# GDN triangular inverses: square transposes on VectorE in place of two trips through DRAM, block matmuls in fixed halves, a shorter queue ahead of them

## The chip, the cores and the metric

The kernel runs on one core of a Trainium2 chip. The metric is the device time of one execution in microseconds (us), lower is better. TensorE (PE) does the matmuls, VectorE (DVE) and ScalarE (ACT) the elementwise work, GpSimd (POOL) a few fills with constants, and SyncE (SP) issues most DMAs. Every engine takes its own instructions in the order in which the program lists them.

## The reference, cut to what matters

Two layers of a flow-matching backbone over 512 latent and 256 context tokens. Each layer has one input projection, three mixers (a convolution module, neighbourhood attention, a gated DeltaNet called GDN), a gated merge and a convolutional feed-forward part. The change touches only the GDN, which is computed chunk by chunk, in two directions and for 4 heads:

```python
diff = g[..., :, None] - g[..., None, :]
decay = jnp.where(incl, jnp.exp(jnp.where(incl, diff, 0.0)), 0.0)
kb = k * beta
lmat = jnp.where(strict, jnp.einsum("bhnid,bhnjd->bhnij", kb, k) * decay, 0.0)
sol = lax.linalg.triangular_solve(lmat, rhs, left_side=True, lower=True, unit_diagonal=True)
```

The reference solves with a unit triangular matrix for each chunk, head and direction. The kernel works with chunks of 128 tokens and computes the inverse of each such 128x128 matrix, which the scan over the chunks then multiplies with.

## The kernel before

The program is written once per layer, and a planner then lists each engine's instructions in an order of its own, from the data that each needs and from the order in which the code was written. `issue_after(x)` adds an edge: what is written inside, on x's engine, is listed behind x.

**The GDN stage.** `gdn_core` is called twice in each layer, for two heads each time. In this document A0 and B0 are the two calls of layer 0, A1 and B1 those of layer 1. One call does the following in turn:

- For each head: matmuls `kk` (k with k) into PSUM, decay tiles `D` on VectorE and ScalarE, then `E` = kk times beta times D on VectorE (24 units in E: 2 directions, 2 heads, 6 chunks), and `A` = qk times D.
- `gdn_inverse(E)`: each unit of E is a 128x128 triangular matrix with four diagonal blocks of 32x32, each 32 partitions by 32 columns. These blocks go out to DRAM (L1031) and come back with one block per partition in `Eb` (L1032 to L1034). VectorE inverts them by a recursion of 31 pairs of instructions (`Tm` L1041, `Tt` L1043) on 112 partitions. The inverses are copied into transposed order (L1046 to L1048), go out to DRAM (L1050, L1051) and come back as 32x32 blocks into `Td` and `E` (L1058, L1059); ScalarE copies some into `TA` (L1060).
- Then block matmuls put the 32x32 inverses together to 64x64 (`iy` L1069, copied to `Y` by ScalarE, then `it` and `ir`), and those to 128x128 (`iy` L1101, `ir` L1110), with copies by ScalarE and VectorE between.
- The scan over the six chunks (`ch`), with v and k from tiles `tk` that are loaded behind the inverse, `kd` being scaled k. Then the output: norm, transposes `oT`.

**Filler.** Other mixers' projections (`na`, `pjl`, `pjc`) wait in a queue. `self.fill(us)` writes as many of their matmuls as take that many microseconds by a count of columns. `FILL` has these amounts for each place and layer: `e` behind each group of kk, `sub` behind the recursion, `y32` and so on behind the block matmuls, `a` to `d` in the scan, then those in the attention. What is left is written behind the attention, in `finish`. Filler's weights come by SP (`raw`), are rounded by ScalarE (`whi`) and split by VectorE (`wlo`); `nrm` reductions on VectorE and `ev`, `nsq` on ScalarE finish its units.

**Conv taps.** Instructions `ca` on VectorE, from another mixer, may be listed behind the end of the second recursion of a layer (in layer 1 the first ten behind that of the first).

**Buffers.** Tag D has three buffers of 1024 elements in a partition; D, Eb, Tt, Tf and tk share them.

Of the kernel before, what the change touches and what calls it, by code (L numbers as in the profile page):

```python
# [32 lines left out]
FILL = (dict(e=3.5, sub=37.6, y32=1.6, t32=2.5, y64=1.3, t64=1.0, a=0.4, b=0.45, c=0.4, d=0.59, out=1.5, x=3.7, pre=2.5, att=2.1),  # L33
        dict(e=4.1, sub=38.3, y32=1.0, t32=2.5, y64=1.69, t64=1.7, a=0.4, b=0.68, c=0.52, d=0.05, out=1.95, x=2.0, pre=2.08, att=1.41))
# [30 lines left out]
class Net:  # L65
# [955 lines left out]
    def gdn_inverse(self, E):  # L1021

        nc, V, S, T, gp = self.nc, self.nc.vector, self.nc.scalar, self.nc.tensor, self.gp
        de, dt, dR = self.d_e
        Eb = gp.tile([128, 1024], F32, tag="D", name="Eb", bufs=3)
        Tt = gp.tile([128, 1024], F32, tag="D", name="Tt", bufs=3)
        Tf = gp.tile([128, 1024], F32, tag="D", name="Tf", bufs=3)
# [35 lines left out]
        Y = gp.tile([128, 12, 64], F32, tag="Y", name="Y")  # L1063
        blk = lambda q, u, c: E[32 * q:32 * q + 32, u, 32 * c:32 * c + 32]
        yb = self.bank("iy")
        for u in range(12):
            for d in range(2):
                for s, t in prs[d]:
                    T.matmul(yb[32 * t:32 * t + 32, 32 * u:32 * u + 32], blk(s, 12 * d + u, t),  # L1069
                             Td[32 * s:32 * s + 32, 12 * d + u, :], start=True, stop=True)  # L1070
        self.fill(FILL[self.l]["y32"])
        Y1 = Y.rearrange("p a b -> p (a b)")[:, 0:384]
        S.activation(Y1, yb[:, 0:384], AF.Copy, scale=-1.0)
        Yq = lambda t, u: Y1[32 * t:32 * t + 32, 32 * u:32 * u + 32]
        tb, rb = self.bank("it"), self.bank("ir")
        for u in range(12):
            for d in range(2):
                for s, t in prs[d]:
                    if s // 2 == d:
                        T.matmul(tb[32 * t:32 * t + 32, 32 * u:32 * u + 32], blk(t, 12 * d + u, t), Yq(t, u),  # L1080
                                 start=True, stop=True)
                    T.matmul(rb[32 * s:32 * s + 32, 32 * u:32 * u + 32], Yq(t, u), blk(t, 12 * d + u, t),
                             start=True, stop=True)
        self.fill(FILL[self.l]["t32"])
# [446 lines left out]
```

## Time and profile before

| what | value |
|---|---|
| times of three runs | 2586.71, 2596.06, 2603.39 us |
| median | 2596.06 us |
| the profiled execution's own time | 2594.31 us |
| its span | 2592.5 us |
| mean granted TensorE clock | 0.983 |
| TensorE busy | 2494.4 us, 96% |
| VectorE, ScalarE busy | 1851.6, 1067.5 us |

The times of the views are from one profiled execution, counted from the start of its span. "Busy" means that at least one instruction of the engine is under way. Matmuls overlap, so a busy TensorE may still take in a new one only now and then; gaps, in contrast, are sure. [...]

### The profile page before, as it was taken

What the parts mean: (1) busy time and instruction counts of PE and PEld (TensorE: products, weight loads), DVE (VectorE), ACT (ScalarE), POOL (GpSimd) and SP (SyncE); (2) the same over time, 40 slices, a digit from 0 to 9 for tenths busy, and PEclk for the clock granted to TensorE, in tenths of its full rate; (3) what the DMA queues carried; (4) which work ended last, traced back from release to release, by engine and by line L of the source; (5) the groups of instructions that cost most, each with busy time, mean ns of one, the idle gap of its engine ahead of it and who ended that gap; (6) DMA issues with size and microseconds to landing.
All of it is one profiled execution on the core that took longest, in us unless ns stands there. A gap on an engine that the chain in (4) does not pass through costs nothing. (4 is left out here: it accounts for less than half of the span.)

```text
span 2592.5 us, 42262 instructions
## 1 busy us (share of the span) xinstructions
PE 2494.4 (96%) x16079; PEld 2156.6 (83%) x16079; DVE 1851.6 (71%) x4138; ACT 1067.5 (41%) x2159; POOL 8.4 (0%) x32
## 2 busy tenths in 40 slices
PE   6999999989999999999999999998989999999999
PEld 4889898967778888888888898887877778888887
DVE  6675578789679888776656477776768977755463
ACT  4564343445342244223223355634344543533242
POOL 0000000000000000000000000000000000000000
PEclk9999999999999999999999989998999999999999
DMA  7224434353458554453442342343446376322332
GB/s 253 91 76 137 138 99 140 98 177 109 149 186 270 179 176 125 121 161 115 150 135 87 110 141 95 120 134 112 146 125 211 100 251 188 130 90 98 98 98 90
DMA packets 207276, 356.77 MB, mean 138 GB/s; under 512 B 54832, under 2 KB 103200, under 8 KB 206944
## 3 DMA queue, kind: packets, MB, share of 16 engines
q1 hardware_dynamic: 182176, 320.97, 39.3%
q10 hardware_dynamic: 24896, 33.09, 3.6%
q8 instruction: 127, 2.08, 0.3%
q14 instruction: 77, 0.63, 0.1%
HBM read 297.31 MB, written 56.68 MB: 137 GB/s over the span
## 5 line engine op out<-in xcount | busy, mean ns | idle before, releaser
L132 DVE TENSOR_TENSOR wlo<-raw,whi 128x1024 fp32r<-128x1024 f32 (+2 forms) x319 | 385.4, 1209 | 292.3 <-ACT whi L131 289.1
L131 ACT CAST whi<-raw 128x1024 fp32r<-128x1024 f32 (+2 forms) x319 | 331.8, 1041 | 616.2 <-PE dn L150 197.7
L150 PE MATMUL upl<-hl,whi 128*128 128x512 f32 (+1 forms) x728 | 282.4, 389 | 2.4 <-ACT hl L322 1.9
L150 PE MATMUL upl<-ol,whi 128*128 128x512 f32 (+1 forms) x728 | 282.1, 388 | 0.0
L150 PE MATMUL upl<-hl,wlo 128*128 128x512 f32 (+1 forms) x728 | 280.9, 386 | 0.2 <-DVE wlo L132 0.2
L448 PE MATMUL pjl<-hl,whi 128*128 128x512 f32 x512 | 210.6, 411 | 7.6 <-ACT whi L131 7.6
L519 DVE SCALAR_TENSOR_TENSOR ca<-yp,caw,ca 128x783 f32<-128x783 f32 (+1 forms) x240 | 212.9, 887 | 6.7 <-ACT ca L512 4.6
L448 PE MATMUL pjl<-ol,whi 128*128 128x512 f32 x512 | 206.6, 404 | 0.0
L448 PE MATMUL pjl<-hl,wlo 128*128 128x512 f32 x512 | 206.2, 403 | 0.3 <-DVE wlo L132 0.2
L150 PEld LDWEIGHTS upl<-hl,whi 128*128 128x128 f32 x728 | 137.3, 189 | 30.7 <-ACT hl L322 2.1
L150 PEld LDWEIGHTS upl<-ol,whi 128*128 128x128 f32 x728 | 137.5, 189 | 30.0
L150 PEld LDWEIGHTS upl<-hl,wlo 128*128 128x128 f32 x728 | 137.4, 189 | 30.1 <-DVE wlo L132 0.7
L150 PE MATMUL dn<-fll,whi 128*128 128x512 f32 x352 | 139.0, 395 | 0.0
L150 PE MATMUL dn<-fhl,wlo 128*128 128x512 f32 x352 | 139.0, 395 | 0.0
L150 PE MATMUL dn<-fhl,whi 128*128 128x512 f32 x352 | 138.6, 395 | 0.1
L448 PEld LDWEIGHTS pjl<-hl,whi 128*128 128x128 f32 x512 | 97.8, 191 | 29.5 <-ACT whi L131 9.7
L448 PEld LDWEIGHTS pjl<-hl,wlo 128*128 128x128 f32 x512 | 97.6, 191 | 21.6 <-DVE wlo L132 1.2
L448 PEld LDWEIGHTS pjl<-ol,whi 128*128 128x128 f32 x512 | 98.0, 191 | 18.9 <-issue 0.5
L245 DVE CUSTOM_DVE_ANT_1 aj<-at,crows,par 128x512 f32<-128x512 f32 x128 | 93.1, 747 | 27.7 <-DMA at<-ada_t 16.0
L584 PE MATMUL na<-wlo,hl 128*128 128x256 f32 x384 | 108.9, 284 | 0.6 <-DVE wlo L132 0.6
L584 PE MATMUL na<-whi,hl 128*128 128x256 f32 x384 | 109.1, 285 | 0.0
L584 PE MATMUL na<-whi,ol 128*128 128x256 f32 x384 | 109.1, 284 | 0.0
(405 smaller groups left out, 6450.3 us busy)
## 6 DMA issues: line engine op xcount, KB each, us to landing
raw<-w_b SPq DMA_DIRECT2D x88, 512.0 KB
raw<-f_up SPq DMA_DIRECT2D x88, 512.0 KB
at<-ada_t SPq DMA_DIRECT2D x160, 256.0 KB
raw<-w_o SPq DMA_DIRECT2D x32, 512.0 KB
raw<-f_dn SPq DMA_DIRECT2D x32, 448.0 KB
raw<-w_a SPq DMA_DIRECT2D x24, 512.0 KB
mg<-mge ACTq DMA_DIRECT2D x48, 256.0 KB
raw<-w_br SPq DMA_DIRECT2D x24, 512.0 KB
```

What stands on the lines that cost most here:

```text
L131: self.nc.scalar.copy(hi[:, :n], r[:, :n])
L132: self.split = self.nc.vector.tensor_sub(lo[:, :n], r[:, :n], hi[:, :n]).ins
L150: self.nc.tensor.matmul(o, wk[a], x[k][b], start=(k == 0 and i == 0), stop=(k == n - 1 and i == 2))
L245: V.tensor_tensor_reduce(p, w, self.crows[:, r, 4 * h:4 * h + 4], 1.0, m if h else self.p(l, "adab")[:, t:t + 1], ALU.mult, ALU.add, accum ...
L448: self.nc.tensor.matmul(o, wk[a], x[k][b], start=(k == 0 and i == 0), stop=(k == n - 1 and i == 2))
L519: nc.vector.scalar_tensor_tensor(a, y[:, k:k + n], w[:, 31 * c + k:31 * c + k + 1], a, ALU.mult, ALU.add)
L584: self.nc.tensor.matmul(ps[:, :256], x[k][a], wk[b], start=(k == 0 and j == 0), stop=(k == 7 and j == 2))
```

## The change

The diagonal blocks no longer leave the chip. VectorE's transpose turns each 32x32 block of its operand by itself, which is what the blocks need: `Db` collects the diagonal blocks of E with the unit as the inner index (direction 1 through a transpose, direction 0 through a copy by ScalarE), one transpose of 128x1024 gives `Z`, with a unit in each partition. The recursion runs on `Z` and `W` over 128 partitions. Two more transposes give `X` and `Yt`, the inverses and their transposes in block form; the matmuls read them there, and copies put them into E and TA.

The block matmuls run in two halves of six units. A new helper `behind()` puts each group of them, and the filler written between groups (`inv`, 0.9 us each), behind the TensorE instruction written just before. `sub` goes from 37.6 and 38.3 to 22.0. X and Yt take the buffers of Db and Z, and the scan's tk loads take those of W, X and Yt. The tag `Td` of one later tile is renamed `sg`.

```diff
-FILL = (dict(e=3.5, sub=37.6, y32=1.6, t32=2.5, y64=1.3, t64=1.0, a=0.4, ...
-        dict(e=4.1, sub=38.3, y32=1.0, t32=2.5, y64=1.69, t64=1.7, a=0.4, ...
+FILL = (dict(e=3.5, sub=22.0, inv=0.9, t64=1.0, a=0.4, ...
+        dict(e=4.1, sub=22.0, inv=0.9, t64=1.7, a=0.4, ...
...
+    def behind(self):
+        eng = self.nc.tensor.engine
+        last = next((i for i in reversed(self.nc.cur_bb.bb.instructions) if i.engine == eng), None)
+        return self.tc.issue_after(last) if last is not None else ExitStack()
...
-        for b in range(4):
-            nc.sync.dma_start(de[b].rearrange("u (j i) -> j u i", i=32), E[32 * b:32 * b + 32, :, 32 * b:32 * b + 32])
-        nc.sync.dma_start(Eb[0:48], de[:, 0:12, :])
-        nc.sync.dma_start(Tf[64:112], de[:, 12:24, :])
-        V.tensor_copy(Eb[64:112], Tf[64:112, ::-1])
-        nc.sync.dma_start(Tt[0:112], self.A["eye32"][0:112])
+        nc.gpsimd.memset(cube(Db)[:, :, 24:32], 0.0)
+        nc.gpsimd.memset(W, 0.0)
+        nc.gpsimd.memset(W[:, ::33], 1.0)
+        for q in qs:
+            V.transpose(cube(Db)[q, :, 12:24].rearrange("p i u -> p u i"), E[q, 12:24, q])
+            S.copy(cube(Db)[q, :, 0:12].rearrange("p i u -> p u i"), E[q, 0:12, q])
+        V.transpose(Z, Db)
         for j in range(31):
...
         self.fill(FILL[self.l]["sub"])
-        S.copy(Mv[0:48], Tv[0:48].rearrange("p i c -> p c i"))
-        S.copy(Mv[64:112], Tv[64:112].rearrange("p i c -> p c i")[:, ::-1, ::-1])
-        V.tensor_copy(Tf[64:112], Tt[64:112, ::-1])
...
-            nc.sync.dma_start(Td[q], dt[b].rearrange("u (j i) -> j u i", i=32))
-            nc.sync.dma_start(E[q, :, q], dR[b].rearrange("u (j i) -> j u i", i=32))
-            S.copy(TA[q, :, 32 * (b % 2):32 * (b % 2) + 32], Td[q, 12 * d:12 * d + 12, :])
+        X, Yt = sq("X"), sq("Yt")
+        V.transpose(X, W)
+        V.transpose(cube(Yt), Wv.rearrange("p i c -> p c i"))
+        inv, ivt = (cube(Yt), cube(X)), (cube(X), cube(Yt))
...
+            for d in range(2):
+                us = slice(12 * d, 12 * d + 12)
+                (S.copy if d else V.tensor_copy)(E[q, us, q], ivt[d][q, :, us].rearrange("p i u -> p u i"))
+            S.copy(TA[q, :, 32 * (b % 2):32 * (b % 2) + 32], inv[d][q, :, 12 * d:12 * d + 12].rearrange("p i u -> p u i"))
...
+        def wait():
+            with self.behind():
+                self.fill(FILL[self.l]["inv"])
+
+        for u0, u1 in halves:
+            yb = self.bank("iy")
+            with self.behind():
+                for u in range(u0, u1):
+                    for d in range(2):
+                        for s, t in prs[d]:
+                            T.matmul(yb[32 * t:32 * t + 32, 32 * (u - u0):32 * (u - u0) + 32], blk(s, 12 * d + u, t),
+                                     inv[d][qs[s], :, 12 * d + u], start=True, stop=True)
+            S.activation(Y1[:, 32 * u0:32 * u1], yb[:, 0:192], AF.Copy, scale=-1.0)
+            wait()
```

The groups of `it` and `ir`, the second `iy` and the last `ir` are written in the same manner, with `wait()` behind each half of all but the last.

**TensorE, around the first iy of A0.** Before, 464 filler matmuls stand between the last qk and the first iy, and filler stands among the iy:

```order
L584 MATMUL na<-whi,ol_148 128x256
L584 MATMUL na<-whi,hl_149 128x256
L1069 MATMUL iy<-Td,E 32x32
L584 MATMUL na<-wlo,hl_149 128x256
L584 MATMUL na<-whi,ol_150 128x256
L584 MATMUL na<-whi,hl_151 128x256
```

Now 94 stand there (B0 174, A1 136, B1 250; before 453, 433, 349):

```order
L453 MATMUL pjl<-ol_149,whi 128x512
L453 MATMUL pjc<-oc_165,whi 128x256
L453 MATMUL pjl<-hl_148,wlo 128x512
L453 MATMUL pjc<-hc_164,wlo 128x256
L1085 MATMUL iy<-Yt,E 32x32 x2
L1085 MATMUL iy<-X,E 32x32 x2
```

The first iy has moved ahead of most of the filler, and all 24 iy of a half stand together, with six filler matmuls behind them.

**VectorE, from the last E of A0 to the recursion.** Before:

```order
L912 SCALAR_TENSOR_TENSOR E<-kk,beta,D 128x128 x4
L924 TENSOR_TENSOR A<-qk,D 128x256 x2
L592 TENSOR_REDUCE nrm<-nsq 128x4 x2
L132 TENSOR_TENSOR wlo<-raw,whi 128x1024
L488 SCALAR_TENSOR_TENSOR th<-th,pjl 128x512
L488 SCALAR_TENSOR_TENSOR th<-th,pjc 128x256
L132 TENSOR_TENSOR wlo<-raw,whi 128x1024
L1034 COPY Eb<-Tf 48x1024
L132 TENSOR_TENSOR wlo<-raw,whi 128x1024
L1041 TENSOR_TENSOR Tm<-Eb,Tt 112x31
```

Now:

```order
L917 SCALAR_TENSOR_TENSOR E<-kk,beta,D 128x128 x4
L929 TENSOR_TENSOR A<-qk,D 128x256 x2
L1040 STREAM_TRANSPOSE Db<-E 32x12x32 x4
L597 TENSOR_REDUCE nrm<-nsq 128x4
L1042 STREAM_TRANSPOSE Z<-Db 128x1024
L597 TENSOR_REDUCE nrm<-nsq 128x4
L1047 TENSOR_TENSOR Tm<-Z,W 128x31
L132 TENSOR_TENSOR wlo<-raw,whi 128x1024
L1049 TENSOR_TENSOR W<-W,Tm 128x31
```

The transposes follow the last A at once. Behind these rows the rest of A0's recursion stands without a break; in A1, B0 and B1 wlo and nrm stand among its steps.

**ScalarE, ahead of the first Y of A0.** Before:

```order
L594 DMA na_99<-ev 128x256
L1060 COPY TA<-Td 32x12x32
L1073 ACTIVATE Y<-iy 128x384
L955 ACTIVATE kd<-tk_3251,bd 128x128 x2
L1086 COPY TA<-it 32x12x32
L1087 COPY TA<-it 32x12x32
```

Now:

```order
L1064 COPY TA<-X 32x12x32 x2
L1062 COPY E<-Yt 32x12x32
L1064 COPY TA<-Yt 32x12x32
L1062 COPY E<-Yt 32x12x32
L1064 COPY TA<-Yt 32x12x32
L1062 COPY E<-Yt 32x12x32 x2
L1087 ACTIVATE Y<-iy 128x192
L960 ACTIVATE kd<-tk_3099,bd 128x128 x2
L1087 ACTIVATE Y<-iy 128x192
```

Eight copies stand together ahead of the first half's Y, and kd between the two halves.

## Rows read from the trace of the kernel before

**Rows 1.** The page, part 1: TensorE's busy time, share of the span, instructions.

```profile
PE 2494.4 (96%) x16079; PEld 2156.6 (83%) x16079; DVE 1851.6 (71%) x4138; ACT 1067.5 (41%) x2159; POOL 8.4 (0%) x32
```

**Rows 2.** Stages: window, length, busy PE PEld DVE ACT POOL, clock, DMA, GB/s.

```profile
229.70:300.90 71.20, 67.41 (x467) 62.05 (x466) 44.38 (x109) 22.93 (x36) 0.09 (x1) 1.00 0.46 134
300.90:322.90 22.00, 20.92 (x444) 19.13 (x444) 4.52 (x10) 9.25 (x22) 0.00 (x0) 1.00 0.54 148
374.10:441.40 67.30, 65.95 (x457) 61.04 (x457) 53.62 (x123) 20.32 (x31) 0.00 (x0) 1.00 0.40 118
441.40:458.00 16.60, 11.50 (x355) 10.49 (x355) 12.96 (x16) 6.65 (x15) 0.00 (x0) 0.79 0.69 187
1687.20:1757.70 70.50, 63.78 (x436) 58.69 (x435) 52.87 (x124) 24.12 (x41) 0.95 (x1) 0.95 0.47 138
1757.70:1774.10 16.40, 9.89 (x336) 9.08 (x336) 3.33 (x6) 6.58 (x14) 0.00 (x0) 0.50 0.70 198
1824.90:1894.40 69.50, 63.73 (x353) 55.20 (x352) 54.03 (x115) 21.31 (x28) 0.00 (x0) 1.00 0.49 146
1894.40:1916.00 21.60, 19.17 (x377) 16.06 (x377) 4.47 (x8) 7.79 (x16) 0.15 (x2) 0.84 0.60 170
sum 355.10, PE 322.35 PEld 291.73 DVE 230.19 ACT 118.95 POOL 1.20; mean PE 40.29 PEld 36.47 DVE 28.77 ACT 14.87 POOL 0.15
```

**Rows 3.** Timeline of VectorE at the end of A0's E: start, length, instruction.

```profile
226.87 1.11 DVE L912 SCALAR_TENSOR_TENSOR E<-kk,beta,D 128x128 f32<-128x128 f32 x4
...
238.32 0.74 DVE L924 TENSOR_TENSOR A<-qk,D 128x256 f32<-128x256 f32 x2
```

**Rows 4.** Timeline of TensorE in A0: last qk, the 94th filler, first iy.

```profile
229.10 0.28 PE L584 MATMUL na<-whi,hl 128*128 128x256 f32 x1
229.22 0.28 PE L584 MATMUL na<-wlo,hl 128*128 128x256 f32 x1
229.33 0.60 PE L920 MATMUL qk<-qT,kT 128*128 128x128 f32 x4
...
245.24 0.27 PE L448 MATMUL pjc<-hc,wlo 128*128 128x256 f32 x1
...
300.92 0.22 PE L1069 MATMUL iy<-Td,E 32*32 32x32 f32 x2 [2.16 <-issue]
```

**Rows 5.** VectorE by line, 243 to 301: xcount, busy, mean ns, idle before.

```profile
L1043 DVE TENSOR_TENSOR Tt<-Tt,Tm 112x31 f32<-112x31 f32 (+15 forms) x31 | 10.6, 342 | 0.9
L1041 DVE TENSOR_TENSOR Tm<-Eb,Tt 112x31 f32<-112x31 f32 (+15 forms) x31 | 10.6, 341 | 0.9
L132 DVE TENSOR_TENSOR wlo<-raw,whi 128x1024 fp32r<-128x1024 f32 x8 | 9.8, 1222 | 11.5 <-ACT whi L131 11.5
L592 DVE TENSOR_REDUCE nrm<-nsq 128x4 f32<-128x256 f32 x4 | 1.7, 416 | 3.5 <-ACT nsq L590 3.5
L1034 DVE COPY Eb<-Tf 48x1024 f32<-48x1024 f32 x1 | 0.7, 692 | 0.0
```

**Rows 6.** Timelines of VectorE and TensorE in A1: last E, the 136th filler.

```profile
1695.74 1.12 DVE L912 SCALAR_TENSOR_TENSOR E<-kk,beta,D 128x128 f32<-128x128 f32 x4
...
1705.29 0.39 PE L448 MATMUL pjl<-hl,whi 128*128 128x512 f32 x1
1705.52 0.39 PE L448 MATMUL pjl<-ol,whi 128*128 128x512 f32 x1
```

**Rows 7.** The same columns as rows 2, over B1's it and ir matmuls alone.

```profile
1908.20:1910.65 2.45, 1.86 (x144) 1.64 (x144) 0.00 (x0) 0.66 (x2) 0.00 (x0) 1.00 0.05 16
```

**Rows 8.** ScalarE's copies into TA: count, duration min/median/max in ns.

```profile
L1060 ACT COPY TA<-Td x16: 507/510/517, 300.8 to 1907.1; 32x384 f32<-32x384 f32 x16
```

**Rows 9.** As rows 2: A0's scan, and the attention of layers 0 and 1.

```profile
322.90:352.90 30.00, 29.98 (x240) 29.11 (x241) 22.64 (x73) 16.50 (x57) 0.00 (x0) 1.00 0.25 81
508.10:700.00 191.90, 182.94 (x1255) 144.36 (x1254) 161.16 (x331) 90.58 (x211) 0.41 (x6) 0.97 0.41 134
1962.00:2100.00 138.00, 130.05 (x854) 99.25 (x853) 117.89 (x293) 72.46 (x153) 0.31 (x4) 0.99 0.51 169
```

More of the change, by code (lines that the diff above doesn't have):

```diff
@@ L31 @@
 TAP_SPLIT = ((0, 0, 20), (10, 10, 40))
[L33 to L34 removed]
+FILL = (dict(e=3.5, sub=22.0, inv=0.9, t64=1.0, a=0.4, b=0.45, c=0.4, d=0.59, out=1.5, x=3.7, pre=2.5, att=2.1),
+        dict(e=4.1, sub=22.0, inv=0.9, t64=1.7, a=0.4, b=0.68, c=0.52, d=0.05, out=1.95, x=2.0, pre=2.08, att=1.41))
 K_ID, K_S1024, K_S32, K_N = 0, 128, 160, 192
@@ L1023, in gdn_inverse @@
         nc, V, S, T, gp = self.nc, self.nc.vector, self.nc.scalar, self.nc.tensor, self.gp
[L1024 to L1027, printed above, removed]
+        sq = lambda name: gp.tile([128, 1024], F32, tag="D", name=name, bufs=3)
+        cube = lambda t: t.rearrange("p (a b) -> p a b", b=32)
+        qs = [slice(32 * b, 32 * b + 32) for b in range(4)]
@@ L1064, in gdn_inverse @@
         blk = lambda q, u, c: E[32 * q:32 * q + 32, u, 32 * c:32 * c + 32]
-        yb = self.bank("iy")
-        for u in range(12):
+        Yq = lambda t, u: Y1[32 * t:32 * t + 32, 32 * u:32 * u + 32]
+        v = lambda x: x.rearrange("p (u c) -> p u c", c=32)
+        halves = [(6 * hh, 6 * hh + 6) for hh in range(2)]
+        def wait():
[11 more added lines that the diff above has]
+            wait()
@@ new lines, in gdn_inverse @@
+        for u0, u1 in halves:
+            tb, rb = self.bank("it"), self.bank("ir")
+            with self.behind():
+                for u in range(u0, u1):
+                    c = 32 * (u - u0)
+                    for d in range(2):
+                        for s, t in prs[d]:
+                            if s // 2 == d:
+                                T.matmul(tb[32 * t:32 * t + 32, c:c + 32], blk(t, 12 * d + u, t), Yq(t, u),
+                                         start=True, stop=True)
+                            T.matmul(rb[32 * s:32 * s + 32, c:c + 32], Yq(t, u), blk(t, 12 * d + u, t), start=True, stop=True)
+            S.copy(TA[32:64, u0:u1, 0:32], v(tb[32:64, 0:192]))
+            S.copy(TA[64:96, u0:u1, 32:64], v(tb[64:96, 0:192]))
@@ L1067, in gdn_inverse @@
             for d in range(2):
                 for s, t in prs[d]:
[L1069 to L1084, printed above, removed]
@@ L1085, in gdn_inverse @@
-        v = lambda x: x.rearrange("p (u c) -> p u c", c=32)
-        S.copy(TA[32:64, :, 0:32], v(tb[32:64, 0:384]))
-        S.copy(TA[64:96, :, 32:64], v(tb[64:96, 0:384]))
-        for d in range(2):
-            for s, t in prs[d]:
-                V.tensor_copy(E[32 * s:32 * s + 32, 12 * d:12 * d + 12, 32 * t:32 * t + 32], v(rb[32 * s:32 * s + 32, 0:384]))
+                    V.tensor_copy(E[32 * s:32 * s + 32, 12 * d + u0:12 * d + u1, 32 * t:32 * t + 32],
+                                  v(rb[32 * s:32 * s + 32, 0:192]))
@@ L1092, in gdn_inverse @@
+            wait()
         Y2 = gp.tile([128, 12, 64], F32, tag="Y", name="Y2")
@@ L1094, in gdn_inverse @@
         w = lambda x: x.rearrange("p (u c) -> p u c", c=64)
-        ybs, rbs = [], []
-        for hh in range(2):
+        for u0, u1 in halves:
             yb = self.bank("iy2")
-            for u in range(6 * hh, 6 * hh + 6):
-                for d in range(2):
-                    s, t = st(d)
-                    T.matmul(yb[t, 64 * (u - 6 * hh):64 * (u - 6 * hh) + 64], E[s, 12 * d + u, t], TA[s, u, :],
-                             start=True, stop=True)
-            S.activation(Y2[:, 6 * hh:6 * hh + 6, :], w(yb[:, 0:384]), AF.Copy, scale=-1.0)
-        self.fill(FILL[self.l]["y64"])
-        for hh in range(2):
-            rb = self.bank("ir2")
-            for u in range(6 * hh, 6 * hh + 6):
-                for d in range(2):
-                    s, t = st(d)
-                    T.matmul(rb[s, 64 * (u - 6 * hh):64 * (u - 6 * hh) + 64], Y2[t, u, :], E[t, 12 * d + u, t],
-                             start=True, stop=True)
+            with self.behind():
+                for u in range(u0, u1):
+                    for d in range(2):
+                        s, t = st(d)
+                        T.matmul(yb[t, 64 * (u - u0):64 * (u - u0) + 64], E[s, 12 * d + u, t], TA[s, u, :],
+                                 start=True, stop=True)
+            S.activation(Y2[:, u0:u1, :], w(yb[:, 0:384]), AF.Copy, scale=-1.0)
+            wait()
+        for u0, u1 in halves:
+            rb = self.bank("ir2")
+            with self.behind():
+                for u in range(u0, u1):
+                    for d in range(2):
+                        s, t = st(d)
+                        T.matmul(rb[s, 64 * (u - u0):64 * (u - u0) + 64], Y2[t, u, :], E[t, 12 * d + u, t],
+                                 start=True, stop=True)
             for d in range(2):
                 s, t = st(d)
-                V.tensor_copy(E[s, 12 * d + 6 * hh:12 * d + 6 * hh + 6, t], w(rb[s, 0:384]))
+                V.tensor_copy(E[s, 12 * d + u0:12 * d + u1, t], w(rb[s, 0:384]))
         self.fill(FILL[self.l]["t64"])
```

24 lines of the change are left out of this document (9 added, 15 removed).

## The prediction, on record before the result was known

> **What bounds the kernel now.** I read the page first. TensorE is busy 96% of the span, 98 us short of all of it [rows 1]. So what the kernel takes is TensorE's work plus its gaps, and a change that leaves its work alone (here: the same matmuls in the same number) can only move the gaps and the clock.
>
> Second view, the table by stage: each of the four inverses (layer 0 pairs A0 and B0, layer 1 pairs A1 and B1) cut in two. The first window of each runs from the last kk or qk matmul to the first block matmul iy; the reader is to see 71, 67, 71 and 70 us in which TensorE has nearly no gap. The second holds the block matmuls, 16 to 22 us. Over all eight, 355.10 - 322.35 = 32.8 us of gaps [rows 2]. That is all that can be won from gaps here. The granted clock adds a little: 16.6 us at 0.79, 16.4 at 0.50, 21.6 at 0.84 and 70.5 at 0.95 lose 3.5 + 8.2 + 3.5 + 3.5 = 18.7 us against the full level [rows 2].
>
> Third, the timelines, for who is late. In A0 the last A, which follows the last E on VectorE, is done at 239.06 [rows 3]; the first iy starts at 300.92 [rows 4]. These 62 us are the path of the old inverse: two trips through DRAM and the recursion. TensorE doesn't notice, since 464 queued matmuls stand in its order between the last qk and the first iy. An engine takes its instructions in order, so this count decides.
>
> **The change part by part.**
>
> *The path to iy gets shorter.* The trips, three copies of 48 partitions and the landing times go. What is left is a sum on VectorE, by the new order in A0: 4 transposes of 32x12x32, one nrm, one transpose of 128x1024, one nrm, one wlo, the 62 recursion steps, two transposes of 128x1024. The steps are 10.6 + 10.6 us busy and 1.8 us of gaps, 23.0 [rows 5]; they have 128 partitions in place of 112 and the same elements in each. nrm is 0.42, wlo 1.22 [rows 5]. No trace shows a square transpose: from below 0.69, the copy of 1024 elements, from above twice wlo; I take 1.15 for 1024 elements, just under wlo (as many elements, but one source in place of two) [rows 5], and 0.43 for 384. A0: 1.7 + 0.8 + 1.15 + 1.2 + 23.0 + 2.3 = 30.2 us from 239.06, so iy could start at 269.2, not 300.9. [...]
>
> *The queue in front gets shorter still.* FILL's sub goes from 37.6 and 38.3 to 22.0, and all block matmuls now stand behind the TensorE instruction written before them, so the planner can't pull filler of a later call ahead of iy within a unit. The new order has 94, 174, 136 and 250 filler matmuls between the last kk or qk and iy, where 464, 453, 433 and 349 stood. In A0 the orders of TensorE and VectorE are the same until the last E, so the trace of before says where TensorE will be: its 94th filler matmul starts at 245.24, done issuing at about 245.4 [rows 4]. It then waits for the transposes: 269.2 - 245.4 = **23.9 us idle**.
>
> A1 likewise: the last E is done at 1696.86, and TensorE has issued its 136 at about 1705.3 [rows 6]. The sum there has 7 nrm and 3 wlo: 1.7 + 2.9 + 1.15 + 3.7 + 23.0 + 2.3 = 34.7, so iy at 1731.6: **26.3 us idle**.
>
> In the B pairs the order ahead of the last E moves too, so I count from the last kk of the pair's first head. From there to the last A took 239.06 - 226.9 = 12.2 us in A0 (the first head's last E group starts at 226.87) [rows 3], and I use that. B0: 6 nrm and 4 wlo give 35.5, together 47.7; TensorE has 246 filler matmuls and 14 of kk and qk ahead of iy, 32.9 + 3.0 = 35.9 us (0.12 us for 256 columns, 0.23 for 512, the starts in [rows 4, 6]; 0.21 for a kk or qk, which the trace shows as two records: four records in 0.60 us end to end, and a new one each 0.11 [rows 4]): **11.8 us idle**. B1: 6 nrm, 3 wlo and a gate step of 0.7, 35.1, together 47.3, against 39.6 us of queue (275 filler matmuls and 10 of kk and qk): **7.7 us idle**. Together 69.7 us; small VectorE steps that also stand in the recursion (a tap, na_finish's thirteen) are left out and could only lengthen it.
>
> *Block matmuls in halves with filler between.* The gaps of the old second windows (1.1, 5.1, 6.5 and 2.4 us [rows 2]) go: while ScalarE moves one half out, TensorE has the other half and 1 us of filler. All 72 it and ir matmuls, 144 records, take 2.45 us [rows 7]; there are as many now, in the same order of blocks, so I add nothing for halving. One wait is added: eight copies into TA and E stand ahead of the first Y copy on ScalarE, 8 x 0.51 = 4.1 us [rows 8] and 0.3 for Y itself, against 0.8 + 1.0 + 0.8 + 1.0 = 3.6 us of TensorE's own work. About 1 us each time, 4 in all. Behind them stands kd, which needs the tk loads; their buffers are now the transposes' own, so SP issues them later. If a load lands after 5 us, the second Y copy is late by the excess; I cost it at nothing, since the filler of two more blocks stands behind.
>
> *The filler isn't saved, only moved.* It comes back in the chunk scan after the inverse, and behind the GDN part. In before the scan ran 30.0 us with 29.98 busy [rows 9]: no gap there to take it.
>
> *The sum:* 69.7 + 4 - 32.8 = +40.9 us. On the profiled execution (2594.31, its span 2592.5, 1.75 below the median of 2596.06) that is 2635.2; on the median 2637.0. I forecast **2637**.
>
> *The clock* I set at nothing: the four new block stages of some 14 us lose 3 each at 0.79, as one did, or 7 each at 0.50, as another did after its gaps [rows 2], 12 to 28 against 18.7 now: -7 to +9. [...]
>
> **The rivals.**
>
> *The path is hidden after all: faster.* If the queue in front covered the path, all 32.8 us of gaps and the 18.7 us of clock would be won: 2545. This decides at idle 0 in the four first windows. For it speaks that the path loses 32 us in A0. Against it: the 23.0 us of recursion alone [rows 5] cannot start before 239 in A0 nor end before 262, and TensorE is through its queue at 245.4 [rows 4].
>
> *The moved filler fills later gaps: no change.* TensorE has 9.0 us of gaps in layer 0's attention and 8.0 in layer 1's [rows 9]. If filler that comes later closed all of it, and the B pairs' idle didn't happen because VectorE is ahead there, the sum is 40.9 - 17 - 19.5 = +4: 2600; with either alone 2617 to 2620. For it speaks that some 30 us of filler now stand around layer 0's start of attention. Against it: those gaps wait for VectorE's softmax steps, and the filler set there per step is unchanged.
>
> *Worse than the sum.* If a transpose costs twice my price (5.2 us more in each inverse, 21) and the clock stays at 0.50 in the block stages (+9), with 10 us for what I left out: 2677.
>
> **How the numbers follow.** One per cent of 2596 is 26 us, about what can be told from no change: below 2570 is faster, above 2622 slower. My forecast's case, 2622 to 2677, has 0.66; the worse case beyond it 0.08; no change 0.19; faster 0.07. So faster 0.07, same 0.19, slower 0.74. The range goes down to 2605 (transposes at 0.69 give -8, the clock -7, later gaps closed -17) and up to 2677.
>
> **What would show it.** Right: TensorE in A0 and A1 idle for 20 to 30 us ahead of the first iy, ended by VectorE's Yt or X; less in B0 and B1; block stages of 14 to 17 us with 1 or 2 us of gaps; the transposes of 1024 elements at 0.7 to 1.3 us; the first iy of A0 near 269. Wrong: no such wait ahead of iy (the order doesn't hold on the chip, or VectorE's path is much shorter), or waits that appear as forecast while the gaps of the attention vanish. If transposes take over 2 us, only the size is off.

## The result, and the profile after

The changed kernel takes 2627.44 us (median of four runs, 2620.26 to 2636.10) against 2595.16 for the kernel before in the same comparison: a ratio of 1.012, 95% interval 1.0099 to 1.0141. It is **slower by 1.2%**, some 32 us. The profiled execution took 2636.1 us, its span 2634.2; it is the slowest of the four.

The first row to read is TensorE's, which answers to [rows 1].

```profile
PE 2485.9 (94%) x16079; PEld 2148.1 (82%) x16079; DVE 1884.2 (72%) x4190; ACT 1081.7 (41%) x2195; POOL 10.4 (0%) x40
```

As many matmuls as before. The span less TensorE's busy time is 2634.2 - 2485.9 = 148.3 us; it was 98.1. So 50 us of gaps have come, and the busy time fell by 8.5. The table by stage tells where. It has the windows of [rows 2]: A0, B0, A1, B1, each from the last kk or qk to the first iy and from there to the scan (window, length, then busy time of PE, PEld, DVE, ACT, POOL, granted clock, DMA share, GB/s).

```profile
232.20:273.90 41.70, 16.79 (x93) 14.21 (x92) 39.20 (x99) 10.32 (x16) 1.11 (x2) 0.72 0.11 38
273.90:291.30 17.40, 17.34 (x393) 14.74 (x394) 9.07 (x19) 10.07 (x20) 0.00 (x0) 0.88 0.53 152
366.40:403.60 37.20, 26.70 (x174) 24.02 (x172) 35.27 (x82) 11.06 (x20) 1.11 (x2) 0.92 0.23 75
403.60:421.10 17.50, 17.38 (x396) 14.98 (x397) 16.96 (x27) 10.91 (x21) 0.00 (x0) 0.88 0.52 168
1707.00:1754.20 47.20, 19.77 (x141) 18.50 (x142) 43.79 (x110) 12.94 (x23) 1.43 (x3) 0.73 0.21 70
1754.20:1778.10 23.90, 21.98 (x396) 17.05 (x397) 15.69 (x27) 11.68 (x22) 0.00 (x0) 0.82 0.41 133
1836.90:1879.40 42.50, 32.62 (x251) 31.33 (x249) 40.86 (x109) 14.31 (x26) 1.11 (x2) 0.92 0.26 85
1879.40:1901.90 22.50, 20.84 (x398) 16.57 (x399) 21.58 (x36) 11.26 (x22) 0.00 (x0) 0.93 0.36 113
sum 249.90, PE 173.43 PEld 151.40 DVE 222.43 ACT 92.55 POOL 4.76; mean PE 21.68 PEld 18.92 DVE 27.80 ACT 11.57 POOL 0.60
```

Length less PE in the four first windows is 24.9, 10.5, 27.4 and 9.9 us, together 72.7; VectorE is busy there for all but 1.6 to 3.4 us. In the four second windows it is 0.1, 0.1, 1.9 and 1.7, together 3.8. The sum of gaps is 76.5 where it was 32.8 [rows 2]: 43.7 of the 50.2 us stand here.

Who ended the wait in A0 is in the timelines. TensorE (start, length, instruction, idle time before it and what ended it):

```profile
247.81 0.80 PE L453 MATMUL pjl<-hl,wlo 128*128 128x512 f32 x1 [2.04 <-DVE wlo L132]
...
251.66 0.27 PE L453 MATMUL pjc<-hc,wlo 128*128 128x256 f32 x1
273.91 0.26 PE L1085 MATMUL iy<-Yt,E 32*32 32x32 f32 x2 [21.98 <-DVE Yt L1054]
```

VectorE, the path that ended it:

```profile
240.44 0.75 DVE L929 TENSOR_TENSOR A<-qk,D 128x256 f32<-128x256 f32 x2
241.11 3.50 DVE L1040 STREAM_TRANSPOSE Db<-E 32x384 f32<-32x384 f32 x4
...
244.98 1.24 DVE L1042 STREAM_TRANSPOSE Z<-Db 128x1024 f32<-128x1024 f32 x1
...
246.43 0.19 DVE L1047 TENSOR_TENSOR Tm<-Z,W 128x31 f32<-128x31 f32 x1
...
270.59 0.19 DVE L1049 TENSOR_TENSOR W<-W,Tm 128x31 f32<-128x31 f32 x1
270.82 1.25 DVE L1053 STREAM_TRANSPOSE X<-W 128x1024 f32<-128x1024 f32 x1
271.99 1.87 DVE L1054 STREAM_TRANSPOSE Yt<-W 128x1024 f32<-128x1024 f32 x1
```

From the last A's end (241.2) to iy it is 32.7 us, where 62 were needed before [rows 3, 4]. VectorE's part of the change does what it says; TensorE was given even less to do meanwhile.

### The profile page after: what moved, and what is told of

Its sections match the earlier page's. It is cut to its first block, busy times and chain, and to the rows that moved or that the text cites. A ratio compares the mean times of both kernels' runs of the same rounds, so it can differ in the third digit from the quotient of the medians.

```text
span 2634.2 us, 42216 instructions
## 1 busy us (share of the span) xinstructions
PE 2485.9 (94%) x16079; PEld 2148.1 (82%) x16079; DVE 1884.2 (72%) x4190; ACT 1081.7 (41%) x2195; POOL 10.4 (0%) x40
## 4 chain that ended last, share of the span: by engine, by line
PE 59%; DVE 14%; DMA 7%; ACT 3%; issue 2%; SPq 0%; ACTq 0%; DVEq 0%; POOL 0%
PE upl L150 18%; PE dn L150 10%; PE pjl L453 6%; PE upc L150 5%; DVE ca L524 4%; PE mbl L150 3%; PE na L589 3%; PE pjl L150 3%; DVE wlo L132 2%; PE og L623 1%; PE wo L150 1%; DMA at<-ada_t 1%; PE pjc L453 1%; DMA mg<-mge 1%; DVE W L1049 1%
## 5 line engine op out<-in xcount | busy, mean ns | idle before, releaser
L453 PE MATMUL pjl<-hl,whi 128*128 128x512 f32 x512 | 216.5, 423 | 4.0 <-ACT whi L131 4.0
L245 DVE CUSTOM_DVE_ANT_1 aj<-at,crows,par 128x512 f32<-128x512 f32 x128 | 93.3, 747 | 32.6 <-DMA at<-ada_t 17.7
```

The source lines that it names most:

```text
L245: V.tensor_tensor_reduce(p, w, self.crows[:, r, 4 * h:4 * h + 4], 1.0, m if h else self.p(l, "adab")[:, t:t + 1], ALU.mult, ALU.add, accum ...
L453: self.nc.tensor.matmul(o, wk[a], x[k][b], start=(k == 0 and i == 0), stop=(k == n - 1 and i == 2))
```

## The experiments

Ratios are to the kernel before on the same chip, with 95% intervals. "Gap" is a window's length less TensorE's busy time.

**The queue's length alone.** The changed kernel with the old numbers in FILL:

```diff
-FILL = (dict(e=3.5, sub=22.0, ...        dict(e=4.1, sub=22.0, ...
+FILL = (dict(e=3.5, sub=37.6, ...        dict(e=4.1, sub=38.3, ...
```

> The changed kernel with one thing undone: sub is 37.6 and 38.3 again, as in the kernel before; the transposes, the halves and the fixed order stay. Between the last kk or qk and the first iy then stand 208, 303, 253 and 273 filler matmuls (A0, B0, A1, B1), where the changed kernel has 94, 174, 136 and 250; by columns 31.9, 40.5, 35.0 and 46.0 us in place of 14.8, 24.4, 17.6 and 31.6. Theory Q (the loss is TensorE's idle ahead of iy, and that idle is the path on VectorE less the queue in front): idle falls from 24.9, 10.5, 27.4 and 9.9 to about 8, 0, 10 and 0 us, 55 us are won, and the time is about 2572. Rival T (the transposes, the strided copies or the halves cost the time themselves, and the queue only shows it): about 2627 as in the changed kernel, at best 2610. Rival M (filler that is taken ahead is missing later, in the scans and in the attention): the idle ahead of iy falls as in Q, but gaps of 20 us or more appear behind it, and the time is 2590 to 2600.

Measured: 2576.13, ratio 0.9918 (0.9892 to 0.9944). The first windows, columns as above:

```profile
228.20:274.60 46.40, 33.26 (x211) 29.37 (x210) 44.07 (x108) 15.81 (x23) 1.12 (x2) 0.91 0.28 93
363.30:408.50 45.20, 42.12 (x306) 39.46 (x304) 42.91 (x98) 17.95 (x29) 1.12 (x2) 1.00 0.30 102
1675.70:1724.50 48.80, 36.45 (x256) 33.71 (x254) 46.49 (x114) 16.59 (x29) 1.43 (x3) 0.95 0.32 103
1807.20:1856.90 49.70, 46.76 (x280) 41.02 (x279) 46.84 (x108) 23.02 (x33) 1.11 (x2) 1.00 0.35 114
```

Gaps 13.1, 3.1, 12.4, 2.9: 31.5 us in place of 72.7, and 51 us less time. Q expected 8, 0, 10 and 0; the waits that end at iy itself are 12.2, 0, 8.4 and 0, the rest are smaller waits within the queue. One entry of FILL turned the loss of 1.2% into a gain of 0.8%. Theory Q stands, T falls: transposes, halves and edges together are faster than what they replaced. M falls too: outside these windows the profile has 70.9 us of gaps, the changed kernel's 75.6. The gaps of these windows are 41 of the 51 us. In the profiles TensorE's busy time fell as well, from 2485.9 to 2468.6 us; some 6 us of that are a stretch at half speed, described in the last section, that one profile has and the other hasn't.

**The path's length alone.** The changed kernel with X and Yt computed three times over:

```diff
+        for _ in range(3):
-        V.transpose(X, W)
-        V.transpose(cube(Yt), Wv.rearrange("p i c -> p c i"))
+            V.transpose(X, W)
+            V.transpose(cube(Yt), Wv.rearrange("p i c -> p c i"))
```

> The changed kernel with X and Yt computed three times over (the same result), which adds 2 x (1.24 + 1.87) = 6.2 us to VectorE's path ahead of iy in each inverse and nothing else. Theory Q: TensorE waits there in all four pairs, so each microsecond of path is one of time: +25, 2652. Rival: if something else bounds the inverses (ScalarE's copies, the loads, filler that is due later), less than 10 us: 2627 to 2637.

Measured: 2646.80, ratio 1.0214 (1.0189 to 1.0239). Against the changed kernel that is 19 us by the medians, and 0.0094 of 2595, 24 us, by the ratios. The first windows of A0 and A1:

```profile
231.30:279.30 48.00, 17.41 (x101) 14.76 (x101) 45.48 (x105) 10.35 (x16) 1.12 (x2) 0.71 0.10 35
...
1712.60:1764.80 52.20, 18.48 (x139) 17.32 (x137) 49.83 (x115) 12.78 (x22) 1.43 (x3) 0.72 0.21 63
```

Gaps 30.6 and 33.7, up by 5.7 and 6.3 for 6.2 us of path; in B0 and B1 they are up by 5.6 and 5.8, together 23.3 us. While TensorE waits there, a microsecond of path is a microsecond of time, from the other side than the queue.

**The transposes taken back.** The kernel with sub 37.6 and 38.3, the diagonal blocks through DRAM again. The halves and the edges stay, but for the edge of the first half's iy, which goes; as many filler matmuls stand in front of it:

```diff
-        for q in qs:
-            V.transpose(cube(Db)[q, :, 12:24].rearrange("p i u -> p u i"), E[q, 12:24, q])
-            S.copy(cube(Db)[q, :, 0:12].rearrange("p i u -> p u i"), E[q, 0:12, q])
-        V.transpose(Z, Db)
+        for b in range(4):
+            nc.sync.dma_start(de[b].rearrange("u (j i) -> j u i", i=32), E[32 * b:32 * b + 32, :, 32 * b:32 * b + 32])
+        nc.sync.dma_start(Eb[0:48], de[:, 0:12, :])
...
-            with self.behind():
+            with (self.behind() if u0 else ExitStack()):
...
-                                     inv[d][qs[s], :, 12 * d + u], start=True, stop=True)
+                                     Td[qs[s], 12 * d + u, :], start=True, stop=True)
```

> The kernel of the run before with sub 37.6 and 38.3 (2576 us), in which the transposes alone are taken back: the diagonal blocks go through DRAM again as in the kernel before, the halves and the edges stay (the first iy has none, but as much filler in front: 208, 303, 253 and 273 matmuls). Theory Q with the path: the path from the last A to iy is some 62 us in place of 33, so iy comes about 25 to 29 us later in each pair, the queue in front covers no more than before, and idle ahead of iy grows by 25 to 29 us in A0 and A1 and by 15 to 25 in B0 and B1, 80 to 105 us in all: 2655 to 2680. Rival D (the trips are hidden anyway, and the transposes give nothing beside halves and edges): 2576 to 2590.

Measured: 2659.97, ratio 1.0269 (1.0236 to 1.0302). The first windows of A0 and B0:

```profile
227.80:295.40 67.60, 32.99 (x212) 29.38 (x211) 38.35 (x102) 14.27 (x20) 0.13 (x1) 0.78 0.35 104
385.80:449.60 63.80, 42.14 (x307) 39.47 (x305) 48.39 (x113) 14.61 (x24) 0.00 (x0) 0.87 0.39 117
```

Gaps 34.6 and 21.7 (29.6 and 20.1 in layer 1), with the very queue of the run with sub 37.6 and 38.3. In A0 33.8 us of them are one wait ahead of iy, which the DMA into Td ends. Behind a queue of this length the transposes are worth 84 us by the medians, 91 by the ratios. Rival D falls. The ratio says too what halves and edges do without the transposes: 2.7% slower than the kernel before, in which 464 and 453 filler matmuls stand where 208 and 303 stand here. The halves were in no run taken back by themselves.

**The trips with a queue long enough for them**, in layer 0:

```diff
-        self.fill(FILL[self.l]["sub"])
+        self.fill(FILL[self.l]["sub"][pr])
...
+FILL = (dict(e=3.5, sub=(66.0, 58.0), ...        dict(e=4.1, sub=(40.0, 36.0), ...
```

> The trips through DRAM with the halves and the edges (all of them), and a queue that is long enough for the trips in layer 0 alone: sub 66 and 58 there, 61.5 and 62.8 us of filler in front of iy by columns; 40 and 36 in layer 1 (36.7 and 43.6). Layer 0, from the first xT to the first upl, took 837.5 us in the kernel before, 831.9 with transposes and sub 37.6, and 875.7 with trips and sub 37.6. Theory Q: what counts is the path less the queue, so layer 0 takes 830 to 842 here, though the path is 30 us longer: where filler covers the trips the transposes give next to nothing. Layer 1 stays near the 659 of the run with trips and sub 38.3. In all about 2620. Rival P (the trips cost by themselves, through DMA or the extra copies): layer 0 at 850 or more.

Measured: 2669.02, ratio 1.0282 (1.0250 to 1.0313). A miss: layer 0 took 868.5 us (118.9 to 987.4), not 830 to 842. (The kernel before took 834.6 to its first upl, not the 837.5 of the expectation.) Its windows ahead of iy (A0, B0), then from the start of the attention to the first lnT, a matmul of the convolution module's norm, and from there to the first upl:

```profile
230.30:301.60 71.30, 63.95 (x437) 58.54 (x437) 43.70 (x108) 21.66 (x32) 0.18 (x1) 0.99 0.44 131
397.70:461.80 64.10, 64.10 (x408) 57.61 (x406) 51.04 (x105) 18.35 (x26) 0.00 (x0) 1.00 0.48 137
569.20:720.50 151.30, 123.75 (x878) 99.87 (x878) 131.53 (x253) 61.47 (x141) 0.41 (x6) 0.93 0.41 132
720.50:987.40 266.90, 246.05 (x1433) 204.67 (x1433) 215.61 (x543) 93.33 (x178) 0.00 (x0) 0.98 0.63 199
```

The idle ahead of iy went as Q has it (gaps 7.4 and 0.0). But the third window has 27.6 us of gaps, and 16.8 of them are one wait. TensorE's row, then the conv taps of layer 0 on VectorE here and in the run with transposes and sub 37.6 (count, ns min/median/max, first and last start):

```profile
720.53 1.09 PE L542 MATMUL lnT<-kc,lnx 128*128 128x128 f32 x4 [16.76 <-DMA lnx<-ca]
...
L525 DVE SCALAR_TENSOR_TENSOR ca<-yp,caw,ca x120: 1015/1029/1036, 444.6 to 714.1; 128x783 f32<-128x783 f32 x120
...
L524 DVE SCALAR_TENSOR_TENSOR ca<-yp,caw,ca x120: 1014/1028/1036, 399.4 to 655.1; 128x783 f32<-128x783 f32 x120
```

The taps stand behind the second recursion, and that ends 45 us later here. Their result comes back as lnx, and TensorE, which is through with what stands in front at 703.8, waits for it until 720.5; in the other run it reaches lnT at 713.6 and finds it there. Filler is not what was missing: 192 filler matmuls of this layer still stand behind the wait. Another 8.8 us of gaps in the last window are waits of wo for wlo. So a queue can cover a long path ahead of iy, and the path still costs: it holds up what VectorE has to do behind it. The time that rival P named (layer 0 at 850 or more) came; that the DMAs or the extra copies cost it by themselves, the rows don't show. No run had lnT behind the filler, which would settle how much of the miss this wait is.

**The edges alone.** `behind()` returns no edge, sub stays at 22.0:

```diff
-        return self.tc.issue_after(last) if last is not None else ExitStack()
+        return ExitStack()
```

> The changed kernel without the edges: behind() adds none, sub stays 22.0. The planner then pulls filler of later calls ahead of iy by itself: 271, 271, 310 and 296 filler matmuls stand there, 42.6, 37.1, 41.6 and 40.0 us by columns, and only 1.5 to 3.7 us of filler are left among the block matmuls (8 to 12 us with the edges). Theory Q: hardly any idle ahead of iy (0, 0, 3 and 2 us), but the gaps among the block matmuls come back, as many as in the kernel before (15 us) and up to 5 us more in each pair, since eight copies on ScalarE stand ahead of the first Y: 2627 - 68 + 11 to 31, that is 2570 to 2590. Rival T: about 2627 or more. If the pin is what loses the time, and not the number in FILL, this run and not the next shows it.

Measured: 2584.91, ratio 0.9949 (0.9930 to 0.9968). The loss turns into a gain of 0.5%, with the small number in FILL still there: the planner pulls other filler ahead of iy (271 to 310 matmuls), and the waits for iy are 0.9 to 1.6 us. So it is the edges that make the number count at that place. The block matmuls pay, as expected: in A0's and B0's second windows

```profile
278.40:294.80 16.40, 10.49 (x348) 9.90 (x349) 8.14 (x18) 9.99 (x19) 0.00 (x0) 0.69 0.47 144
390.40:402.80 12.40, 9.63 (x353) 9.06 (x354) 10.57 (x21) 9.60 (x20) 0.00 (x0) 0.86 0.50 155
```

there are 5.9 and 2.8 us of gaps (2.0 and 2.3 in layer 1); with the edges 0.1 and 0.1 (1.9 and 1.7).

**The small number without edges and transposes**, in the kernel before:

```diff
-FILL = (dict(e=3.5, sub=37.6, ...        dict(e=4.1, sub=38.3, ...
+FILL = (dict(e=3.5, sub=22.0, ...        dict(e=4.1, sub=22.0, ...
```

> The kernel before with sub = 22.0 and nothing else. In its planner's order 464, 453 and 433 filler matmuls still stand between the last qk and the first iy in A0, B0 and A1, as before, and 419 in B1 (349). Theory Q, in which the number of matmuls that stand there decides: no change, 2590 to 2600, and the first iy of A0 at 300 to 302 us. Rival S (the smaller number alone shortens the queue and loses time): 2610 to 2650.

Measured: 2640.54, ratio 1.0166 (1.0144 to 1.0189). A miss in the time: 2590 to 2600 was expected. At the place that Q speaks of nothing changed: first iy of A0 at 298.9, gap 2.95. The loss comes later. Layer 0, from its first xT to its first upl, takes 849.8 us where it took 834.6, layer 1 665.2 where it took 628.9; 9 us are won between the two. The windows: A0 ahead of iy, from B0's scan to the attention, from B1's scan to the attention, layer 1's attention.

```profile
228.30:298.90 70.60, 67.65 (x468) 62.24 (x467) 44.45 (x110) 22.96 (x36) 0.16 (x1) 1.00 0.45 135
...
488.80:526.90 38.10, 30.73 (x181) 26.64 (x180) 32.72 (x70) 13.37 (x40) 0.20 (x3) 0.96 0.47 150
...
1949.30:1974.90 25.60, 8.07 (x35) 5.75 (x33) 22.98 (x64) 5.66 (x21) 0.16 (x2) 0.67 0.34 113
1974.90:2121.50 146.60, 132.68 (x840) 103.13 (x841) 100.96 (x248) 65.58 (x139) 0.16 (x2) 0.94 0.44 146
```

The three last in the kernel before, whose first iy of A0 was at 300.92 [rows 4]:

```profile
488.20:524.50 36.30, 35.89 (x210) 31.04 (x209) 32.51 (x69) 13.47 (x40) 0.20 (x3) 1.00 0.46 149
...
1945.10:1971.40 26.30, 26.07 (x121) 21.07 (x119) 25.94 (x66) 10.19 (x27) 0.00 (x0) 1.00 0.52 181
...
1971.40:2081.70 110.30, 103.06 (x718) 77.67 (x719) 96.23 (x245) 58.70 (x129) 0.31 (x4) 0.98 0.46 151
```

The window between B1's scan and the attention holds 35 matmuls and 17.5 us of gaps, where 121 left 0.2. The planner, given less to put in front, took what stood there (419 ahead of B1's iy in place of 349), and TensorE waits for VectorE: 9.6 us for the attention's `ax`, 7.9 for the scaling of the scan's output. Behind B0 it is the same in small, 181 matmuls and 7.4 us of gaps, one wait for `ax`, where 210 left 0.4. Rival S has the size by a way that it didn't name. Why layer 1's attention then has 13.9 us of gaps in place of 7.2 (it also holds 122 more matmuls) stays open.

**Strides.** Db unit by unit, so that the small transposes write in one piece and Z reads with steps; then X and Yt too:

```diff
-            V.transpose(cube(Db)[q, :, 12:24].rearrange("p i u -> p u i"), E[q, 12:24, q])
-        V.transpose(Z, Db)
+            V.transpose(cube(Db)[q, 12:24, :], E[q, 12:24, q])
+        V.transpose(cube(Z), cube(Db).rearrange("p u i -> p i u"))
...
-        V.transpose(X, W)
-        V.transpose(cube(Yt), Wv.rearrange("p i c -> p c i"))
+        V.transpose(cube(X).rearrange("p u i -> p i u"), Wv)
+        V.transpose(cube(Yt).rearrange("p u c -> p c u"), Wv.rearrange("p i c -> p c i"))
```

> The changed kernel with the diagonal blocks collected unit by unit (each 32x32 result in one piece of memory), and the stride moved into the one transpose that makes Z. In the changed kernel the four transposes into Db (384 elements, writes 128 bytes apart) take 0.85 to 0.89 us each, those of 1024 elements in one piece 1.24, and Yt, which reads 128 bytes apart, 1.87. Theory stride (the step in memory costs): the four fall to about 0.46 (384/1024 of 1.24), ScalarE's copies into Db from 0.90 to about 0.5, and Z rises to about 1.87; in all 1.0 us less path in each inverse and iy as much earlier, 2627 - 4, not to be told from no change in time. Rival (small transposes have a fixed price): the four stay at 0.85 and more, Z rises, the path is 0.6 longer.

> The run above, and X and Yt are written unit by unit too, so that the copies into E and TA and the matmuls read in one piece, and the transposes carry every stride. Theory stride: X rises from 1.24 to about 1.87 (writes apart), Yt (both apart) from 1.87 to 2.5, ScalarE's eight copies fall from 0.85 to 0.51 (as the copies into TA from Td in the kernel before), VectorE's four from 0.67; the first Y copy starts some 2.7 us sooner behind iy. The block stages have hardly a gap in the changed kernel (0.1, 0.1, 1.9 and 1.7 us), so the time changes by less than 5 us: 2622 to 2632. Rival (the copies ahead of Y do hold TensorE up): 3 us won in each pair, 2615.

Measured: one run each, 2618.13 and 2622.71, not to be told from the changed kernel's 2620 to 2636. VectorE's groups in A0 of the second (line, engine, operation, count, busy us, mean ns, idle before):

```profile
L1040 DVE STREAM_TRANSPOSE Db<-E 32x384 f32<-32x384 f32 x4 | 2.3, 568 | 0.0
L1042 DVE STREAM_TRANSPOSE Z<-Db 128x1024 f32<-128x1024 f32 x1 | 2.0, 1984 | 0.0
L1054 DVE STREAM_TRANSPOSE Yt<-W 128x1024 f32<-128x1024 f32 x1 | 1.9, 1917 | 0.0
L1053 DVE STREAM_TRANSPOSE X<-W 128x1024 f32<-128x1024 f32 x1 | 1.9, 1907 | 0.0
L1062 DVE COPY E<-X 32x384 f32<-32x384 f32 x4 | 1.4, 340 | 0.1
```

The step in memory does cost: the small transposes fell from 0.87 to 0.57 (0.46 was expected), X rose from 1.25 to 1.91, Z from 1.24 to 1.98; ScalarE's copies fell from 0.85 to 0.51. But Yt, with steps on both sides, takes 1.92, as with one: 2.5 was wrong. In the first run the path is shorter by 1.2 - 0.74 = 0.5 us, in the second longer by 0.2. The time doesn't answer, which fits.

**Looking for a faster version.** First sub for each pair; then sub 38 with the strides of the run above; then both, with numbers between:

```diff
+FILL = (dict(e=3.5, sub=(46.0, 34.0), ...        dict(e=4.1, sub=(48.0, 33.0), ...
...
+FILL = (dict(e=3.5, sub=(42.0, 35.0), ...        dict(e=4.1, sub=(43.0, 33.0), ...
```

> The changed kernel with sub set for each pair: 46 and 34 in layer 0, 48 and 33 in layer 1 (22 for all in the changed kernel). The queue in front of iy is 41.3, 37.3, 45.1 and 40.8 us by columns, against 39.7, 34.9, 45.0 and 41.5 that the changed kernel's queue and idle make together. Theory Q: idle ahead of iy is at most 3 us in each pair, some 70 us are won, and the time is about 2557, faster than the kernel before by 1.4%. Rival T: about 2627. Rival M: 2590 to 2600, with the gaps moved behind.

> Two things together: sub 37.6 and 38.3 (2576 us by itself), and Db, X and Yt written unit by unit (shorter copies; by the profile of that run the path to iy is about as long: four transposes 0.57 in place of 0.87, ScalarE's copies 0.51 in place of 0.85, but Z 1.98 in place of 1.24 and X 1.91 in place of 1.25). Theory Q: iy waits in A0 and A1 as it does with sub alone, 8 to 10 us each; the shorter copies lie behind gaps of under 1 us; no difference from sub alone: 2570 to 2580, 0.992 of the kernel before. Rival (the copies hold up something after all): 2565 or less.

> The same with sub set for each pair between the two earlier tries: 42 and 35 in layer 0, 43 and 33 in layer 1, 42.4, 37.7, 39.9 and 40.5 us of filler in front of iy by columns. Theory Q alone: idle ahead of iy about 0, 0, 5 and 1 us, 15 us less than with 38 for all: 2560. Rival M (what is taken in front in A is missing behind, as in the run with 46, 34, 48, 33, which was expected at 2557 and took 2584): 2575 to 2585.

Measured: 2584.25, ratio 0.9948 (0.9929 to 0.9966); 2576.47, 0.9923 (0.9903 to 0.9942); 2569.72, 0.9895 (0.9873 to 0.9917). The strides give nothing beside the queue, as expected. The last lies between what Q (2560) and M (2575 to 2585) said of it and is the fastest kernel of the study, about 1% faster than the kernel before. Its windows ahead of iy in A0 and A1 have gaps of 3.7 and 7.0 us:

```profile
229.40:277.50 48.10, 44.38 (x293) 39.80 (x292) 45.46 (x109) 16.09 (x29) 1.12 (x2) 1.00 0.31 104
...
1680.40:1730.60 50.20, 43.24 (x300) 39.77 (x298) 46.93 (x114) 15.33 (x31) 1.43 (x3) 0.95 0.32 105
```

The first was expected at 2557, since its gaps ahead of iy would go; 27 us are missing. The gaps fell to 4.3, 3.3, 5.5 and 2.4 us, of which 1.5, 0.9, 0 and 0 are waits for iy: 57 us fewer, not 70. Two of its windows, A1 ahead of iy and from layer 1's attention to upl:

```profile
1683.50:1738.70 55.20, 49.73 (x343) 46.27 (x341) 51.48 (x121) 22.48 (x37) 1.43 (x3) 0.95 0.36 115
...
2066.50:2212.20 145.70, 135.93 (x817) 116.92 (x816) 110.36 (x223) 64.23 (x107) 0.00 (x0) 0.96 0.64 204
```

In A1 the queue itself is now the longer: 343 matmuls in 49.7 us, and iy comes 5 us later than with 300. In the second window the gaps are 9.8 us; in the changed kernel that stretch has 4.7. Outside the four windows ahead of iy the profile has 79.6 us of gaps, the changed kernel's 75.6, that with sub 37.6 and 38.3 70.9. So rival M has the direction, with 4 to 9 us. The 13 us that the gaps ahead of iy kept and 4 us elsewhere leave 10 of the 27 us open; the changed kernel's profiled execution, with which these gaps are compared, is 9 us over its median.

**Filler out of the scans.** The fastest kernel with

```diff
-  a=0.4, b=0.45, c=0.4, d=0.59, ... att=2.1        a=0.4, b=0.68, c=0.52, d=0.05, ... att=1.41
+  a=0.0, b=0.45, c=0.0, d=0.0,  ... att=2.75       a=0.0, b=0.68, c=0.0, d=0.0,   ... att=2.05
```

> The fastest kernel so far (2570) with the filler of the scans taken out but for one place in four (a, c and d are 0, b stays) and att raised from 2.1 and 1.41 to 2.75 and 2.05. In the order some 196 and 91 filler matmuls fewer stand among layer 0's and layer 1's scans; layer 1's attention gets 47 more, layer 0's none, the rest stands behind them. Theory C (filler in a scan covers nothing, since the scan of the kernel before ran 30.0 us without a gap with 23 filler matmuls in it): the scans get shorter by what was taken out, with no gaps of their own, and the same matmuls take as long elsewhere: 2565 to 2575, or up to 7 less if layer 1's attention closes its gaps of 7.7 us. Rival S (the scan does need it: its chain over VectorE and ScalarE shows up as gaps): 3 us or more of gaps in each scan, 2580 or more.

Measured: 2570.53, ratio 0.9902 (0.9883 to 0.9921), no change. The scans of A0 and B0, and layer 1's attention:

```profile
291.70:320.70 29.00, 29.00 (x244) 28.81 (x243) 21.34 (x70) 15.04 (x56) 0.00 (x0) 1.00 0.15 48
404.60:437.50 32.90, 32.56 (x273) 31.75 (x272) 29.93 (x91) 16.51 (x58) 0.00 (x0) 1.00 0.07 26
1920.70:2056.00 135.30, 125.61 (x843) 97.52 (x844) 101.85 (x249) 66.53 (x141) 0.26 (x2) 0.97 0.50 163
```

The scans are 7.0 and 15.5 us shorter than before this edit (36.0 and 48.4) and still have hardly a gap (0.0 and 0.3): filler there covers nothing. The attention's gaps (9.7 us, 7.7 before the edit) did not close, though it got more filler.

## Why the prediction was right, and where its terms were off

The forecast was 2637, the result 2627.4; sign and mechanism are as forecast, and runs with the queue and with the path alone show it. The steps:

- **What bounds the kernel.** Held: the matmuls are the same in number, and the time moved by its gaps. TensorE's busy time, which the sum left alone, fell by 8.5 us.
- **The path in A0** was put at 30.2 us; it is 32.7. The recursion is as forecast (24.35 us from the first to the last step, with one wlo of 1.2 in it). The small transposes were mis-sized: 0.87 each, not 0.43, which is 1.8 us; X and Yt took 3.0, not 2.3, since Yt reads with steps. The price of a 1024-element transpose, 1.15, was right only for those in one piece (1.24). With steps of 128 bytes such a transpose took longer: 1.87 us for Yt here, 1.98 for Z and 1.91 for X in the runs on strides.
- **The idle ahead of iy** was forecast (A0, A1, B0, B1) as 23.9, 26.3, 11.8 and 7.7, sum 69.7; the gaps are 24.9, 27.4, 10.5 and 9.9, sum 72.7. In A0 two errors nearly cancel: iy came at 273.9, not 269.2, and TensorE was through its queue at 251.9, not 245.4. Some 2 us of both are the whole timeline being later; 2.9 us of the second are small waits within the queue (24.9 less the 22.0 of the one long wait), which count as gap too; the other 1.5 are matmuls at half speed behind the longer of these waits (a granted clock of 0.50 from 247.8 to 250.6; 0.63 us for 512 columns where it is 0.39 at the full level). That the queue has waits of its own, for its weights, is a step that the prediction left out.
- **The block stages** were put at 4 us; they have 3.8. The reason given holds only in part: ScalarE's copies took 0.85 each, 6.8 us and not 4.1, and the first Y copy started 5.0 us behind iy (278.93 against 273.91), yet layer 0 has gaps of 0.1. The halves and the filler between hid more than was credited; the 3.6 us stand in layer 1.
- **The clock** was set at nothing, -7 to +9. The second windows lose 2.1 + 2.1 + 4.3 + 1.6 = 10.1 us against 15.1 before [rows 2]: -5. The levels of 0.72 and 0.73 in A0's and A1's first windows fall mostly into idle time (0.55 and 0.57 in the long waits for iy) and cost little; the upper end, +9, did not come.
- **Filler is only moved.** Held: A0's scan has 350 matmuls in 45 us, and its gaps are still none. That later gaps would take it up (the rival for "no change") fell: outside the eight windows the gaps rose by 6.5 us.
- **The sum** of gaps is +43.7 measured in the windows against +40.9. That the profiled execution (2636.1; forecast 2635.2) fits to 1 us is in part luck: the gaps outside the windows, +6.5, and the busy time, -8.5, were both put at nothing and nearly cancel. The median is 9 us lower than that execution. Why the runs of one kernel spread by 16 us isn't settled but for one part of it (below).
- **The rival "hidden path"** was priced at 2545 for a queue that covers it. Covering it all but for 6.2 us of waits for iy (sub 42, 35, 43, 33) gave 2570. The price took all gaps and all lost clock of the eight windows, 32.8 and 18.7 us, as won; in that run 17.7 us of gaps still stand there, most of them not waits for iy, and 7.1 us of lost clock. And filler in front isn't free: the tries with more of it have 4 to 9 us more of gaps elsewhere.

## What to carry to other kernels

When a path gets shorter, the work queued in front of its end may shrink by as much as the path did, and by no more: here some 30 us less path, with a queue shorter by more than that, lost 1.2%, where the same path with a queue cut to fit gains 1%. Read both from one view, the end of the path on its engine and the end of the queue on the waiting one; the difference is the idle time, nearly one to one (6.2 us of path gave 5.6 to 6.3). A number that asks for filler holds at its place only where the order is fixed; a planner that is free to move filler may take it from places that need it, and filler put where an engine has no gaps (the scans here) covers nothing. A queue that covers a path doesn't make the path free: what stands behind it on its own engine (here the conv taps) comes later too.
